# First stage of a hybrid encoder layer: mean squares from a second reading of x, and the heads' norm a tile later

## The chip, the cores and the metric

The kernel runs on one core of a Trainium2 chip, with no other core in use. The metric is the device time of one execution in microseconds, lower is better. A core has a matrix engine (TensorE, PE in the profile, with its weight loads as PEld), a vector engine (VectorE, DVE), a scalar engine (ScalarE, ACT), a general engine (GpSimd, POOL), and SyncE (SP), which here only issues transfers. Each engine works off a queue of its own in order, and they meet through semaphores. Sixteen DMA engines move the data between the chip's memory and the on-chip buffers.

## The reference

One layer of an encoder is applied to two sequences, of 2048 and 256 tokens, each token with 1024 values. The part that matters here is its beginning:

```
n = x * rsqrt(mean(x*x) + eps) * norm1_w
p = n @ w_in         # 4 x 512 columns for the matrix memory (mLSTM), 32 gates, 512 + 128 + 128 for q, k, v
q = rmsnorm per head of 64 (q) * q_norm_w ;  k likewise with k_norm_w
q, k = q*cos + rotated(q)*sin, ...             # axial rotary embedding
```

After it follow a bidirectional matrix memory with eight heads, softmax attention with eight query heads and two key heads, an output projection, a second norm, a gated convolution network, and a last norm. All values are float32.

## The kernel before, in words

Tokens are cut into 18 tiles of 128: tiles 16 and 17 belong to the short sequence and come first, then 0 to 15. The first stage is `phase_a`. It makes, for each tile, the attention's q, k and v and the gates (800 columns of w_in). The other columns are projected later, by the matrix memory's part, from a copy of the split x that the first stage leaves in memory.

To keep float32 accuracy with a faster form of the matrix product, every operand is split into a rounded half and a remainder; a product is then three matrix products. x is held transposed (`xT`: values on the partitions, tokens along the row), as the matrix product wants it. It is not normalised before the product: since the norm is one factor for each token, it is multiplied in afterwards, when the accumulators are read.

For one tile, the steps and their lines are:

- `front_a` (L184 to L189): SP issues the load of the transposed x, 512 KB, into one of three buffers.
- `front_b` (L191 to L198): ScalarE copies x into the rounded half (L195), VectorE makes the remainder (L196), and SP stores both, 1 MB (L197). Three tiles of the result `nT` are kept.
- `front_c` (L200 to L213): the mean square of each token. ScalarE squares x (L204), GpSimd adds the eight blocks of 128 values in three steps (L207 twice, L208), TensorE multiplies the sum by a vector of ones (L210), which adds over the partitions and puts the result on the tokens, VectorE adds eps (L212), GpSimd raises to the power -1/2 (L213). The result is a column of `g.rc`.
- `mm` (L244 to L258): 48 matrix products into an accumulator tile `pj` of two banks, of which there are two.
- `post_a` (L260 to L278): ScalarE reads q and k out of the accumulators with the token's factor (L264) into `qk`, of which there are two, and v (L267); VectorE makes v's remainder (L268) and the gates (L272); SP stores v (L270). ScalarE squares q and k (L275), VectorE sums for each head (L277), GpSimd adds eps and raises to -1/2 (L104, L105 in the helper `rstd_of`).
- `post_b` (L280 to L303): VectorE multiplies by the head's factor (L283) and applies the rotation in seven operations (L292, L296, L298), ScalarE and VectorE split the result (L300, L301), SP stores the queries (L302).
- `post2` (L332 to L338): TensorE turns the two key halves (L336), ScalarE copies them out (L337) and stores them from its own queue (L338).
- `gates` (L305 to L330): the forget gates' logarithms, for some tiles at a time, and their turn on TensorE (L329).

The loop at L357 sets the order in which the program is written. In iteration n it has `mm` of tile n, `post2` of tile n-1, `post_a` of n, `front_b` and `front_c` of n+3, `post_b` of n, some gate steps, some of the rotation's tables (`tables2`, on GpSimd, L241), one part of the next stage's weights (`wm`), and the load of x for n+4. A block under `tc.issue_after(ins)` adds, for each of its instructions on the engine of `ins`, that it is issued behind `ins`. The order in which each engine's queue is finally laid out comes from the framework's scheduler, which follows the written order as priority, but brings forward what it takes to be ready. After the loop come `gate_math`, the matrix memory's projections (`mj` at L780, `mv` at L790) and the attention, which are interleaved. The accumulators `pj` of the first stage make room for those of the projections.

Two parts of the matrix memory's code serve as rows for costs: L941 squares with a running sum on ScalarE, and L777 loads the stored split x back.

Of the kernel before, what the change touches and what calls it, by code (L numbers as in the profile page):

```python
# [9 lines left out]
F32 = mybir.dt.float32  # L10
F32R = mybir.dt.float32r
AF = mybir.ActivationFunctionType
# [141 lines left out]
def phase_a(g, tc, sw, st_x, after_x, after_mm, after_pj, wm):  # L154
# [3 lines left out]
    with ExitStack() as st:  # L158
# [32 lines left out]
        def front_b(i):  # L191

            nT = nTs[i] = sf.tile([P, NCC, 2, P], F32R, tag="nT", name=f"n1T{i}", bufs=3)
            x = xs[i]
            nc.scalar.activation(nT[:, :, 0, :], x, AF.Copy)  # L195
            ins = nc.vector.tensor_tensor(nT[:, :, 1, :], x, f32(nT[:, :, 0, :]), ALU.subtract)  # L196
            g.st.dma_start(g.n1_d[i // 2, :, :, i % 2], f32(nT))  # L197
            return ins  # L198

        def front_c(i):  # L200

            x = xs.pop(i)
            xq = sx.tile([P, NCC, P], F32, tag="xq", name=f"xq{i}", bufs=2)
            nc.scalar.activation(xq, x, AF.Square, scale=1.0 / 32.0)  # L204
            sq = sf.tile([P, P], F32, tag="sq", name=f"sq{i}")
            for k in (4, 2):
                nc.gpsimd.tensor_tensor(xq[:, 0:k], xq[:, 0:k], xq[:, k:2 * k], ALU.add)  # L207
            nc.gpsimd.tensor_tensor(sq, xq[:, 0], xq[:, 1], ALU.add)  # L208
            ps = pp.tile([P, 2], F32, tag="rs", name=f"rs_a{i}", bufs=2)
            nc.tensor.matmul(ps, sq, g.ones, start=True, stop=True)  # L210
            r = g.rc[:, i:i + 1]
            nc.vector.tensor_scalar(r, ps[:, 0:1], EPS, None, ALU.add)  # L212
            nc.gpsimd.tensor_tensor(r, r, g.mhalf[:, 0:1], ALU.pow)  # L213

        def weights(cs):
# [44 lines left out]
        def post_a(i, pj):  # L260

            qk = sp.tile([P, 10, HD], F32, tag="qk", name=f"qk{i}")
            rc = g.rc[:, i:i + 1]
            nc.scalar.activation(qk, pj[:, 0:640].rearrange("p (h d) -> p h d", d=HD), AF.Copy, scale=rc)  # L264
            v = sp.tile([P, 2, 2, HD], F32R, tag="v", name=f"v{i}", bufs=2)
            pv = pj[:, 640:768].rearrange("p (h d) -> p h d", d=HD)
            nc.scalar.activation(v[:, 0], pv, AF.Copy, scale=rc)  # L267
            nc.vector.scalar_tensor_tensor(v[:, 1], pv, rc, f32(v[:, 0]), ALU.mult, ALU.subtract)  # L268
            for a in range(2):
                g.st.dma_start(g.v_d[a, :, :, i].rearrange("g p d -> p g d"), f32(v[:, a]))  # L270
            gt = g.gtm[:, i]
            nc.vector.scalar_tensor_tensor(gt, pj[:, 768:800].rearrange("p (a k) -> p a k", a=2), rc,  # L272
                                           bgb.rearrange("p (a k) -> p a k", a=2), ALU.mult, ALU.add)
            xq = sp.tile([P, 10, HD], F32, tag="t2", name=f"qkq{i}", bufs=2)
            nc.scalar.activation(xq, qk, AF.Square, scale=0.125)  # L275
            ms = sp.tile([P, 10], F32, tag="ms10", name=f"ms10_{i}")
            nc.vector.tensor_reduce(ms, xq, AX.X, ALU.add)  # L277
            return qk, rstd_of(g, sp, ms, 10, f"rqk{i}")  # L278

        def post_b(i, qk, r):  # L280

# [70 lines left out]
        front_c(order[2])  # L352
        tables2(slice(0, 2))
        front_a(order[3])
        prev = None
        steps = []
        for n, i in enumerate(order):  # L357
            pj, = mm(i)
            if n:
                post2(order[n - 1], prev)  # L360
            if n == NT - 1:
                st_f.close()
                after_mm()
            qk, r = post_a(i, pj)
            with ExitStack() as behind:
                if n + 3 < NT:
                    behind.enter_context(tc.issue_after(front_b(order[n + 3]).ins))
                    front_c(order[n + 3])
                    if n + 4 == NT:
                        st_x.close()  # L370
                        after_x()
                prev = post_b(i, qk, r)
                if steps:
                    for _ in range(2 if n == NT - 1 else 1):
                        next(steps[0], None)
                if n < 7:
                    tables2(slice(2 * n + 2, min(2 * n + 4, NT1)))
                if wm:
                    wm.pop(0)()
            if n + 4 < NT:  # L380
                front_a(order[n + 4])
            if n == NT - 1:
                st_j.close()
                after_pj()
            if n % 4 == 1:
                for _ in (steps.pop() if steps else ()):
                    pass
                steps = [gates(*((NT1, 2) if n == 1 else (i - 3, 4)))]
                next(steps[0])
        for _ in steps[0]:  # L390
            pass
        post2(order[-1], prev)
# [1368 lines left out]
def layout(inputs):  # L1761
# [4 lines left out]
    def col(v):  # L1766
# [4 lines left out]
    w_m = np.concatenate([w_m[:LASTP], w_m[LASTP:][:, :, :, [1, 2, 0, 3]]], axis=0)  # L1771
    arrays = {
        "xT": x.reshape(NT, P, NCC, P).transpose(0, 3, 2, 1),
        "w_a": np.concatenate([w_in[:, ACOL + 32:ACOL + 800], w_in[:, ACOL:ACOL + 32]], axis=1).reshape(NCC, P, 800),
        "w_m": w_m.reshape(4, NCC, P, 512),
        "w_up": inputs["w_up"][0].reshape(NCC, P, 2 * NFC, P).transpose(2, 1, 0, 3),
# [26 lines left out]
```

## Time and profile before

| what | value |
|---|---|
| median of three runs | 3371.0 us (3368.56 to 3371.91) |
| span of the profiled execution, the one time that is shown of it | 3372.4 us |
| TensorE busy, whole span | 97% |
| first projection of the first stage starts | 8.35 us |
| first projection of the matrix memory (L780) starts | 208.21 us |
| mean granted TensorE clock, whole span | 0.986 |

The profile is that of one execution. A row of a busy-time view gives a stretch's bounds, then for each engine the microseconds it was busy and the number of instructions, the mean clock that TensorE was granted (1.00 is full), the share of the DMA engines that was busy, and the rate. A row of the waits names who waited, for what, then the total, how often, and the longest, in microseconds. A row of the groups gives line, engine, operation, output and inputs, shapes and count, then the total busy time and the mean of one in nanoseconds, then the idle time before it and who ended it. A row of the order of time gives start, length, engine, line, and in brackets the idle time of the engine before it. A row on one source line gives shortest, middle and longest duration in nanoseconds, then the first and last start.

### The profile page before, as it was taken

What the parts mean: (1) busy time and instruction counts of PE and PEld (TensorE: products, weight loads), DVE (VectorE), ACT (ScalarE), POOL (GpSimd) and SP (SyncE); (2) the same over time, 40 slices, a digit from 0 to 9 for tenths busy, and PEclk for the clock granted to TensorE, in tenths of its full rate; (3) what the DMA queues carried; (4) which work ended last, traced back from release to release, by engine and by line L of the source; (5) the groups of instructions that cost most, each with busy time, mean ns of one, the idle gap of its engine ahead of it and who ended that gap; (6) DMA issues with size and microseconds to landing.
All of it is one profiled execution on the core that took longest, in us unless ns stands there. A gap on an engine that the chain in (4) does not pass through costs nothing. (4 is left out here: it accounts for less than half of the span.)

```text
span 3372.4 us, 57131 instructions
## 1 busy us (share of the span) xinstructions
PE 3271.5 (97%) x21366; PEld 3047.6 (90%) x21366; DVE 2403.1 (71%) x3727; ACT 1802.4 (53%) x3781; POOL 1327.6 (39%) x1686
## 2 busy tenths in 40 slices
PE   8899999999999999899999999999999999999998
PEld 6788888888888888788889999999999998999998
DVE  7875687777768788876766778877877776544573
ACT  5545666667666777665552544445555555323331
POOL 8652133213333323211246457645554442851112
PEclk9999999999999999999999999999999999999999
DMA  8765343343336444433347334424322223885563
GB/s 273 229 201 150 94 126 97 105 125 98 113 108 188 130 135 128 123 99 96 103 133 263 129 102 148 127 96 176 107 93 97 100 93 102 302 274 172 164 223 107
DMA packets 300636, 483.03 MB, mean 143 GB/s; under 512 B 36597, under 2 KB 186279, under 8 KB 300359
## 3 DMA queue, kind: packets, MB, share of 16 engines
q1 hardware_dynamic: 247543, 348.34, 32.8%
q0 software_dynamic: 36256, 121.60, 10.8%
q10 hardware_dynamic: 16560, 9.44, 0.9%
q8 instruction: 168, 2.75, 0.3%
q14 instruction: 109, 0.89, 0.1%
HBM read 337.37 MB, written 141.91 MB: 142 GB/s over the span
## 5 line engine op out<-in xcount | busy, mean ns | idle before, releaser
L622 DVE TENSOR_TENSOR pl<-ps,ph 128x512 fp32r<-128x512 f32 x520 | 354.0, 685 | 202.1 <-ACT ps L621 190.3
L1226 PE MATMUL pa<-nt,wut 128*128 128x290 f32 (+1 forms) x3168 | 449.2, 298 | 8.7 <-ACT u L1244 8.6
L620 ACT ACTIVATE ph<-ps 128x512 fp32r<-128x512 f32 x520 | 310.0, 596 | 265.7 <-PE ps L617 253.1
L1226 PEld LDWEIGHTS pa<-nt,wut 128*128 128x128 f32 x3168 | 433.1, 190 | 10.9 <-ACT u L1244 10.6
L591 DVE TENSOR_REDUCE mx<-px 128x1 f32<-128x512 f32 (+1 forms) x528 | 346.5, 674 | 100.0 <-PE px L590 98.0
L1336 DVE SCALAR_TENSOR_TENSOR y<-u,cw,y 128x1152 f32<-128x1152 f32 (+1 forms) x176 | 325.3, 1848 | 39.2 <-ACT yc L1334 17.5
L634 PE MATMUL pv<-ph,v 128*128 128x512 f32 (+1 forms) x1040 | 319.4, 402 | 0.8 <-ACT ph L620 0.3
L621 ACT ACTIVATE ps<-ps 128x512 f32<-128x512 f32 x520 | 310.3, 597 | 0.0
L1555 PE MATMUL et<-tet,wet 128*128 128x384 f32 x1584 | 279.0, 336 | 0.0
L1555 PEld LDWEIGHTS et<-tet,wet 128*128 128x128 f32 x1584 | 277.1, 188 | 0.0
L1069 PEld LDWEIGHTS po<-cmx,wo 128*128 128x128 f32 x1728 | 221.6, 191 | 9.6 <-DVE cmx L1057 1.5
L1069 PE MATMUL po<-cmx,wo 128*128 128x256 f32 x1728 | 225.8, 284 | 1.5 <-DVE cmx L1057 1.3
L1555 PE MATMUL e<-te,we 128*128 128x384 f32 x1188 | 213.9, 341 | 11.0 <-ACT te L1397 7.1
L1555 PEld LDWEIGHTS e<-te,we 128*128 128x128 f32 x1188 | 211.5, 191 | 12.0 <-ACT te L1397 7.3
L616 PE MATMUL ps<-qq,kk 128*128 128x512 f32 x520 | 215.9, 417 | 6.0 <-DVE mx L591 3.8
L780 PE MATMUL mj<-mn,wm 128*128 128x256 f32 x1296 | 200.8, 289 | 9.7 <-DMA mn<-n_d 3.9
L780 PEld LDWEIGHTS mj<-mn,wm 128*128 128x128 f32 x1296 | 185.5, 194 | 26.6 <-issue 6.8
L617 PE MATMUL ps<-qm,kl 65*128 65x512 f32 x520 | 207.6, 401 | 0.0
L590 PE MATMUL px<-kk,qq 128*128 128x512 f32 (+1 forms) x528 | 203.2, 415 | 3.9 <-DVE mx L591 2.6
L790 PEld LDWEIGHTS mv<-wm,mn 128*128 128x128 f32 x1296 | 181.9, 190 | 17.8 <-ACT qb L786 2.3
L790 PE MATMUL mv<-wm,mn 128*128 128x256 f32 x1296 | 194.8, 285 | 0.9 <-ACT qb L786 0.8
L634 PE MATMUL pv<-pl,v 128*128 128x512 f32 x520 | 192.2, 401 | 0.0
(307 smaller groups left out, 7216.9 us busy)
## 6 DMA issues: line engine op xcount, KB each, us to landing
mn<-n_d SPq DMA_DIRECT2D x216, 256.0 KB, 3.4
ru<-w_up SPq DMA_DIRECT2D x88, 512.0 KB, 3.6
a_d<-y POOLq DMA_DIRECT2D x88, 288.0 KB, 2.6
a_d<-tc POOLq DMA_DIRECT2D x66, 288.0 KB, 2.8
n_d<-n1T SPq DMA_DIRECT2D x18, 1024.0 KB, 5.7
dm<-nm_d POOLq DMA_DIRECT2D x72, 256.0 KB, 4.0
mjn<-n_d SPq DMA_DIRECT2D x72, 256.0 KB, 3.5
mvn<-n_d SPq DMA_DIRECT2D x72, 256.0 KB, 3.1
```

Of the source, the lines that this page charges most:

```text
L591: nc.vector.tensor_reduce(s.mx[:, t, z0:z0 + 1], ps[:, 0:w], AX.X, ALU.max)
L616: nc.tensor.matmul(ps, kk[:, kc:kc + P], s.qq[:, 0:N], start=True, stop=False)
L620: nc.scalar.activation(ph, ps, AF.Exp)
L621: nc.scalar.activation(ps, ps, AF.Exp)
L622: nc.vector.tensor_tensor(pl, ps, f32(ph), ALU.subtract)
L634: nc.tensor.matmul(s.pv[0:HD if k in (1, 3) else P, 0:N], v, p, start=(kp == 0 and k == 0), stop=(2 * kp + 2 == s.nk and k == 5))
L780: nc.tensor.matmul(pj[:, o], s.w[c][:, a, o * P:(o + 1) * P], nT[c][:, :, h, :], start=(c + o + k == 0), stop=(c == NCC - 1 and k == 2 and ...
L790: nc.tensor.matmul(pv[:, o], nT[c][:, o, a, :], s.w[c][:, h, 256:512], start=(c + o + k == 0), stop=(c == NCC - 1 and k == 2 and o == 1))
L1069: nc.tensor.matmul(po[:, o], wo[z // 2][c][:, a, n], mx[c][:, h, :], start=(c == 0 and k == 0), stop=(c == NCC - 1 and k == 2))
L1226: nc.tensor.matmul(p[:, z], w[:, aa, c, :], ops[k][:, c, bb, z * m:z * m + m], start=c == 0 and i == 0 and not add, stop=c == NCC // 2 - 1 ...
L1336: nc.vector.scalar_tensor_tensor(y[:, s:e], u[:, s + k:e + k], cw[:, k, jj:jj + 1], y[:, s:e], ALU.mult, ALU.add)
L1555: nc.tensor.matmul(ps[m // 2][:, m % 2], w[:, aa, m * P:(m + 1) * P], t[:, bb], start=p == 0 and n == 0, stop=p == NP - 1 and n == 2)
```

## The change

The host also hands in x as it is, token-major (`xn`, 18 tiles of 128 tokens by 1024 values). `front_c` loads that tile on SP's queue (512 KB), ScalarE squares it in place and gives the sum over the row as an accumulated output straight into the column of `g.rc`, and GpSimd adds eps and raises to the power. The three additions of GpSimd, the product with ones and VectorE's addition are gone. x in its transposed form is now read by `front_b` alone.

The loop runs `post_b` of tile n-1 in iteration n, behind the sum over the heads of tile n on VectorE, and `post2` of tile n-2. After the loop the last tile's `post_b` and the last two `post2` follow.

```
         def front_b(i):
...
-            x = xs[i]
+            x = xs.pop(i)
...
         def front_c(i):
-            x = xs.pop(i)
-            xq = sx.tile([P, NCC, P], F32, tag="xq", name=f"xq{i}", bufs=2)
-            nc.scalar.activation(xq, x, AF.Square, scale=1.0 / 32.0)
-            sq = sf.tile([P, P], F32, tag="sq", name=f"sq{i}")
-            for k in (4, 2):
-                nc.gpsimd.tensor_tensor(xq[:, 0:k], xq[:, 0:k], xq[:, k:2 * k], ALU.add)
-            nc.gpsimd.tensor_tensor(sq, xq[:, 0], xq[:, 1], ALU.add)
-            ps = pp.tile([P, 2], F32, tag="rs", name=f"rs_a{i}", bufs=2)
-            nc.tensor.matmul(ps, sq, g.ones, start=True, stop=True)
+            xn = sx.tile([P, D], F32, tag="xn", name=f"xn{i}", bufs=2)
+            nc.sync.dma_start(xn, g.xn[i])
             r = g.rc[:, i:i + 1]
-            nc.vector.tensor_scalar(r, ps[:, 0:1], EPS, None, ALU.add)
+            nc.scalar.activation(xn, xn, AF.Square, scale=1.0 / 32.0, accum_out=r)
+            nc.gpsimd.tensor_scalar(r, r, EPS, None, ALU.add)
             nc.gpsimd.tensor_tensor(r, r, g.mhalf[:, 0:1], ALU.pow)
...
-            nc.vector.tensor_reduce(ms, xq, AX.X, ALU.add)
-            return qk, rstd_of(g, sp, ms, 10, f"rqk{i}")
+            last = nc.vector.tensor_reduce(ms, xq, AX.X, ALU.add)
+            return qk, rstd_of(g, sp, ms, 10, f"rqk{i}"), last.ins
...
-            if n:
-                post2(order[n - 1], prev)
+            if n > 1:
+                post2(order[n - 2], prev)
...
-            qk, r = post_a(i, pj)
+            qk, r, last = post_a(i, pj)
...
-                prev = post_b(i, qk, r)
+                if n:
+                    with tc.issue_after(last):
+                        prev = post_b(order[n - 1], *behind_a)
+                behind_a = qk, r
...
+        post2(order[-2], prev)
+        prev = post_b(order[-1], *behind_a)
         for _ in steps[0]:
             pass
         post2(order[-1], prev)
```

More of the change, by code (lines that the diff above doesn't have):

```diff
@@ L354, in phase_a @@
         front_a(order[3])
-        prev = None
+        prev = behind_a = None
         steps = []
@@ L1773, in layout @@
         "xT": x.reshape(NT, P, NCC, P).transpose(0, 3, 2, 1),
+        "xn": x.reshape(NT, P, D),
         "w_a": np.concatenate([w_in[:, ACOL + 32:ACOL + 800], w_in[:, ACOL:ACOL + 32]], axis=1).reshape(NCC, P, 800),
```

## The prediction

> **What bounds the kernel now.** I read the page first: the span, and the busy shares of the engines.
>
> ```profile
> span 3372.4 us, 57131 instructions
> PE 3271.5 (97%) x21366; PEld 3047.6 (90%) x21366; DVE 2403.1 (71%) x3727; ACT 1802.4 (53%) x3781; POOL 1327.6 (39%) x1686
> ```
>
> TensorE is busy 97% of the span, so over the whole kernel the bound is TensorE and a change pays only where it shortens TensorE's own work or its idle time. The span is the only time that is shown of this profiled execution; it lies 1.4 us (0.04%) above the 3371.0 us median of the three runs, which is small against the steps below, so I make the sum against 3372.4 us and give the result as it comes out. The changed code runs only in the first stage. There I read the busy time by stretch, second.
>
> ```profile
> core 0: us, PE busy (x) PEld busy (x) DVE busy (x) ACT busy (x) POOL busy (x), PEclk, DMA share, GB/s
> 0.00:20.00 20.00, 11.01 (x46) 9.13 (x47) 13.24 (x12) 13.91 (x15) 11.73 (x19) 1.00 0.92 309
> 20.00:60.00 40.00, 36.93 (x193) 31.64 (x192) 27.68 (x54) 18.07 (x26) 35.59 (x47) 0.96 0.87 287
> 60.00:110.00 50.00, 42.50 (x235) 36.86 (x233) 40.31 (x73) 27.72 (x45) 38.83 (x36) 0.97 0.67 214
> 110.00:160.00 50.00, 44.12 (x231) 37.75 (x232) 40.39 (x82) 27.13 (x49) 30.64 (x28) 0.94 0.73 237
> 160.00:205.00 45.00, 44.58 (x257) 38.72 (x255) 36.89 (x78) 22.18 (x44) 25.72 (x27) 0.99 0.67 224
> ```
>
> Three things stand in it. From 20 to 205 us TensorE is idle for 3.07 + 7.50 + 5.88 + 0.42 = 16.9 us. The granted clock takes (1 - 0.96) x 40 + (1 - 0.97) x 50 + (1 - 0.94) x 50 + (1 - 0.99) x 45 = 6.5 us more. And the DMA engines are nowhere idle: their share is 0.87, 0.67, 0.73, 0.67, after 0.92 at the start. After 160 us TensorE hardly waits, so what there is to win lies before. Third I read what ended TensorE's idle time in the first 205 us.
>
> ```profile
> PE rs_a L210 <- POOL sq L208: 6.3, 4, 2.7
> PE pk L336 <- DVE qz L301: 3.7, 3, 1.7
> PE pj L254 <- DVE gtm L320: 3.2, 1, 3.2
> PE pj L254 <- DVE gtm L272: 1.9, 2, 1.6
> PE pg L329 <- ACT kT L337: 1.4, 1, 1.4
> ```
>
> These five are 16.5 of the 16.9 us. The first is the sums of squares: the tiny matmul against ones stands in TensorE's queue behind a projection and waits for GpSimd's additions. The second is the keys' turn waiting for the rotated heads. The next two are a projection that waits until VectorE has read the accumulators of two tiles earlier.
>
> **Removed: the sums of squares on GpSimd and TensorE.** Here are the groups of GpSimd from 20 to 205 us.
>
> ```profile
> L105 POOL TENSOR_TENSOR rqk<-rqk,mhalf 128x10 f32<-128x10 f32 x17 | 37.1, 2181 | 1.0
> L207 POOL TENSOR_TENSOR xq<-xq 128x512 f32<-128x512 f32 x16 | 25.4, 1594 | 7.7 <-ACT xq L204 7.7
> L207 POOL TENSOR_TENSOR xq<-xq 128x256 f32<-128x256 f32 x16 | 16.7, 1051 | 0.6
> L213 POOL TENSOR_TENSOR rc<-rc,mhalf 128x1 f32<-128x1 f32 x17 | 15.4, 908 | 19.0 <-DVE rc L212 19.0
> L104 POOL TENSOR_SCALAR rqk<-ms 128x10 f32<-128x10 f32 x17 | 11.3, 664 | 24.0 <-DVE ms L277 23.5
> L208 POOL TENSOR_TENSOR sq<-xq 128x128 f32<-128x128 f32 x16 | 10.0, 630 | 0.6
> ```
>
> The three additions cost 1.594 + 1.051 + 0.630 = 3.3 us for each tile, 52 us over the stretch. They go, and a small addition of 128x1 comes in, between 0 and the 0.66 us of the 128x10 one; I take 0.5 us. GpSimd is off TensorE's path once nothing on TensorE waits for it, so its 2.8 us a tile count through the waits alone: the 6.3 us go entirely, because the matmul itself goes. That matmul's own slots go too.
>
> ```profile
> 77.48 0.28 PE L210 MATMUL rs_a<-ones,sq 128*128 128x2 f32 x2
> 77.62 2.11 PE L254 MATMUL pj<-w_a,n1T 128*128 128x512 f32 x8
> ```
>
> From its start to that of the next projection is 0.14 us, where it waited for nothing. Eighteen tiles make 2.5 us of TensorE time, all on the path.
>
> GpSimd's additions also cost VectorE time.
>
> ```profile
> L283 DVE TENSOR_TENSOR xh<-qk,rqk x18: 817/826/1918, 43.4 to 218.4; 128x640 f32<-128x640 f32 x18
> DVE xh L283 <- POOL rqk L105: 25.0, 16, 3.6
> ACT qk L264 <- DVE xh L283: 19.0, 8, 5.2
> ```
>
> The multiply by the heads' norm takes 0.82 us, but up to 1.92 us when an addition of GpSimd runs beside it. VectorE also stands 25.0 us waiting for the heads' power on GpSimd, and ScalarE 19.0 us behind that. VectorE is at 145 of 185 us (27.68 + 40.31 + 40.39 + 36.89), so both are what makes it late.
>
> **Moved: norm, rotation and keys' turn a tile later.** Before, VectorE's queue holds norm and rotation of a tile (which wait for GpSimd) ahead of the next tile's reading of its accumulators. Now the reading comes first, then the previous tile's rotation, whose power was finished a tile ago. So the 25.0 us wait goes, the accumulators are released early (3.2 + 1.9 us of TensorE), and the turn stands on TensorE behind a projection more (3.7 us). All that the moved part issues moves with it: nine operations on VectorE, one on ScalarE, the query store on SP's queue, and in the later half two transposes, a copy and a store on ScalarE's queue. Their number is unchanged. What is late next: the buffer of the heads' values has two places, so reading tile n needs the norm of tile n-2, which now runs one iteration closer to it. With VectorE no longer waiting that has most of a tile to spare; if VectorE lags, the 19.0 us row stays. The wait of 1.4 us (a transpose of the gates behind a copy) has no part in it and stays.
>
> **The clock.** The halved clock follows the waits, as two short stretches show.
>
> ```profile
> 61.00:63.50 2.50, 0.00 (x0) 0.00 (x0) 2.50 (x4) 0.00 (x0) 2.50 (x3) 1.00 0.45 143
> 65.00:68.00 3.00, 3.00 (x12) 2.62 (x11) 2.10 (x6) 3.00 (x6) 3.00 (x2) 0.50 0.98 253
> ```
>
> TensorE is idle for the wait of 2.7 us on the squares, and soon after runs at 0.50. If the waits go, the 6.5 us go with them. The Trainium skill, page "TensorE: Matmul & The Clock Gate" (Part 1 and "HAM oscillation"), has the gate fall back after an idle window of about 3.4 us and advises against gaps above that; by it waits of 1.7 to 2.7 us would cost no clock, and of the 6.5 us only those behind the one 3.2 us wait, at most 3.0 us, might go. The rows decide here: a gap below 3 us was followed by half clock.
>
> **The end of the stage.** The matrix-memory projections start late.
>
> ```profile
> 204.48 0.38 PE L329 MATMUL pg<-ident,gp 128*40 128x128 f32 x2
> 205.43 0.36 ACT L267 ACTIVATE v<-pj,rc 128x128 fp32r<-128x128 f32 x1
> 207.72 0.23 DVE L268 SCALAR_TENSOR_TENSOR v<-pj,rc,v 128x128 fp32r<-128x128 f32 x1
> 207.87 0.24 DVE L272 SCALAR_TENSOR_TENSOR gtm<-pj,rc,bgb 128x32 f32<-128x32 f32 x1
> 208.21 1.05 PE L780 MATMUL mj<-mn,wm 128*128 128x256 f32 x4 [3.35 <-issue]
> ```
>
> They begin 0.1 us after VectorE's last reading of the last accumulators, which stood behind the rotation of the tile before. Now that rotation follows it, so it can start at 205.8 instead of 207.7: 1.8 us. On the other side one rotation more (about 6 us of VectorE) now comes after the loop, ahead of the last gates; the projections cover it, since they need neither. If that cover were gone it would cost those 6 us.
>
> **Added: the second reading of x.** ScalarE squares the same 1024 elements, and its running sum must be read out. The trace has that form further down, in the heads' norm of the matrix memory.
>
> ```profile
> L204 ACT ACTIVATE xq<-x 128x1024 f32<-128x1024 f32 x15 | 15.6, 1055 | 11.5 <-POOL sq L208 6.4 <-DMA x<-xT 3.8 <-POOL rqk L104 1.3
> L941 ACT ACTIVATE s<-hh x144: 238/248/311, 443.7 to 1433.7; 128x64 f32<-128x64 f32 x144
> L941 ACT ACTIVATION_READ_ACCUMULATOR s<-hh x144: 187/192/258, 443.8 to 1433.8; 128x1 f32 x144
> ```
>
> So 0.19 us for each tile, 3.5 us on ScalarE in all, hidden: it is busy 95.1 of 185 us. The square no longer waits for GpSimd (6.4 + 1.3 us), but it now waits for a load of its own, with qk, v and everything else of ScalarE queued behind it, and TensorE behind those.
>
> ```profile
> x<-xT SPq DMA_DIRECT2D x16, 512.0 KB, 6.6
> SPq L270 <- ACT v L267: 27.7, 9, 4.6
> 34.46 1.06 ACT L195 ACTIVATE n1T<-x 128x1024 fp32r<-128x1024 f32 x1 [1.59 <-DMA x<-xT]
> ```
>
> The like load of x takes 6.6 us to land. The new one can be issued when its buffer (two places) is free, two tiles ahead; but SP's queue is in order and stands 27.7 us behind the value stores alone. A 524 KB load costs the DMA engines, at the 237 GB/s for a share of 0.73 (325 GB/s for a full one), 1.6 us; eighteen cost 29 us. At the start three of them lie ahead of the fourth tile's x, which ScalarE already waited 1.59 us for: that is 0 to 4.8 us later.
>
> **The sum.** What can go at most from 20 to 205 us is 6.3 + 3.7 + 3.2 + 1.9 of waits, 2.5 of slots and 6.5 of clock: 24.1 us. What the DMA engines allow is less. From 20 to 160 us they are busy 34.8 + 33.5 + 36.5 = 104.8 us; some fifteen new loads add 24: 129 of 140 us, which is the 0.92 of the fullest stretch shown. At that share the stretch does not shrink at all, unless stores slip into the 45 us after it, which have room for (0.92 - 0.67) x 45 = 11 us; then it can shrink by about 12. Between 0 and 12 I take 8, since the stores are what can slip (three tiles of n are kept, and the waits removed came from engines, not from DMA). With 1.8 us at the end the gain is 10 us: 3372.4 - 10 = 3362 us. TensorE being the bound afterwards, it should reach the end of the kernel.
>
> **Rivals.** *The DMA engines take the place of GpSimd* (chance 0.28): the stretch keeps its 140 us, loads of x come late, only the end's 1.8 us and some 2 us after 160 remain: 3368 us, from 3364 to 3374. For it speaks the 0.87 from 20 to 60 us; against it that TensorE's rows name no DMA there.
>
> *ScalarE's queue stands behind the new load* (0.16, the slower side): if SP issues the load only when its own tile's turn comes, ScalarE waits up to 6.6 us a tile. It has 90 us free over the 17 tiles from 20 to 205 us, 5.3 us each; beyond that each microsecond is TensorE's. It decides once load and square together leave less than those 5.3 us: 1.3 us x 17 = 22 us slower, 3394; with the 10 us gained set against it, 3384. Against it: nothing keeps the load from being issued two tiles ahead.
>
> *Nearly everything goes* (0.12): DMA keeps up, 24.1 and the end's 3.35 us go: 3345 us. Against it the DMA sum above.
>
> **Chances.** The forecast case, 3357 to 3366 us, has 0.44. A difference of 0.2%, 6.7 us, is about what a measurement here can tell. Faster than that takes in nearly all of the forecast and the third rival; within it lie most of the DMA rival and the forecast's upper edge: 0.53, 0.31, 0.16. From 3349 to 3376 us the range leaves out most of the last rival and most of the slower one.
>
> **What would show it.** Right: no wait of TensorE on GpSimd in the first stage, 0.99 or more of clock from 60 to 160 us, VectorE's multiply near 0.82 us throughout and not waiting for the power, DMA share above 0.8 there, matrix-memory projections before 200 us. Wrong: ScalarE's square waiting for the second reading for over 20 us in all, or TensorE's projections ending idle time on n1T or on a DMA; then the DMA rival or the slower one holds. Also wrong if the stage ends earlier and the last instruction does not.

## The result and the profile after

The changed kernel takes 3351.6 us (median of four runs, 3349.3 to 3356.0) against 3369.8 us of the kernel before (median of four, 3364.7 to 3371.9). The ratio is 0.9948, with a 95% interval of 0.9936 to 0.9960: 18.2 us, or 0.5%, faster. The forecast was 10 us. The two profiled executions lie further apart than the medians, 3348.6 against 3372.4 us of span, which is 23.8 us: before's profiled execution has a span of 3372.4 us, longer than each of its four timed executions (3371.9 at most). A step by step account within the profiles therefore has to explain 23.8 us, and a statement on the kernels 18.

The head of the page first: span, and busy time, share and instructions of each engine.

```profile
span 3348.6 us, 57051 instructions
PE 3261.4 (97%) x21330; PEld 3037.4 (91%) x21330; DVE 2373.6 (71%) x3709; ACT 1803.6 (54%) x3799; POOL 1267.4 (38%) x1650
```

TensorE has 36 instructions fewer (two passes for each of the 18 products with ones), GpSimd 36 fewer and 60 us less, VectorE 18 fewer. None of that is 24 us of TensorE: its busy time fell by 10.1 us and the span by 23.8, so more than half of it was idle time. The busy time by stretch shows where (columns as in the prediction).

```profile
0.00:20.00 20.00, 12.13 (x52) 9.94 (x53) 11.00 (x11) 12.27 (x13) 2.01 (x13) 1.00 0.91 331
20.00:60.00 40.00, 36.43 (x195) 31.18 (x194) 25.51 (x59) 21.53 (x34) 27.51 (x43) 0.96 1.04 360
60.00:110.00 50.00, 49.30 (x272) 42.73 (x271) 41.56 (x87) 34.43 (x62) 25.80 (x25) 1.00 1.05 368
110.00:160.00 50.00, 49.69 (x284) 43.39 (x284) 38.52 (x90) 33.49 (x62) 22.41 (x23) 1.00 0.93 304
160.00:205.00 45.00, 41.45 (x283) 38.35 (x283) 29.36 (x64) 22.71 (x54) 22.14 (x49) 0.96 0.67 216
```

From 60 to 160 us TensorE is busy 98.99 of 100 us at full clock, where it was busy 86.62 at 0.97 and 0.94. From 20 to 60 us nothing was won: 36.43 us against 36.93. In the first 20 us TensorE is busy 1.1 us more (12.13 against 11.01), which the prediction had not counted. The DMA engines stand at 1.04 and 1.05, above the 0.92 that the prediction took for full. What ended TensorE's idle time in the first 205 us:

```profile
PE pj L248 <- ACT w_a L112: 7.4, 1, 7.4
PE pj L248 <- ACT n1T L195: 2.2, 1, 2.2
PE mj L779 <- ACT og L795: 2.2, 1, 2.2
PE pj L248 <- DVE gtm L266: 1.9, 3, 1.0
PE mv L789 <- ACT qb L785: 1.3, 1, 1.3
```

The first row is the start of the kernel and was there before (8.3 us). No row names GpSimd any more, nor the keys' turn. Two of the rows belong to the matrix memory, which now begins inside this window. In order of time, TensorE's end of the stage:

```profile
178.79 1.58 PE L248 MATMUL pj<-w_a,n1T 128*128 128x288 f32 x10
180.21 1.59 PE L779 MATMUL mj<-mn,wm 128*128 128x256 f32 x12
```

The projection of the matrix memory follows that of the first stage without a gap, at 180.21 us instead of 208.21. These 28.0 us hold the whole gain; 4.2 us of them are lost again by the end of the span. VectorE's waits and its multiply by the heads' factor (min, median, max in nanoseconds, then first and last start):

```profile
DVE xh L277 <- POOL rqk L105: 1.8, 1, 1.8
```

```profile
L277 DVE TENSOR_TENSOR xh<-qk,rqk x18: 811/818/1027, 45.9 to 189.9; 128x640 f32<-128x640 f32 x18
```

The wait for the power fell from 25.0 us to 1.8, and the multiply takes 0.82 us throughout, 1.03 at most, where it took up to 1.92. ScalarE pays for it as follows, in its groups from 20 to 205 us and in its waits of the first 205 us.

```profile
L205 ACT ACTIVATE xn<-xn 128x1024 f32<-128x1024 f32 x17 | 17.9, 1052 | 4.0 <-DMA xn<-xn 2.6 <-ACT kT L331 0.9 <-DMA rm<-w_m 0.4
L205 ACT ACTIVATION_READ_ACCUMULATOR xn<-xn 128x1 f32 x17 | 3.2, 188 | 0.0
```

```profile
ACT n1T L195 <- DMA x<-xT: 3.3, 3, 2.7
ACT xn L205 <- DMA xn<-xn: 2.9, 4, 2.1
ACT qk L258 <- DVE xh L277: 1.1, 1, 1.1
```

The running sum costs 0.19 us a tile, as the row from the matrix memory said. ScalarE waits for the second reading four times, 2.9 us in all, and its 19.0 us behind the multiply are 1.1.

### The profile page after: what moved, and what is told of

Same layout as the page of the kernel before. It is cut to its first block, busy times and chain, and to the rows that moved or that the text cites. A ratio compares the mean times of both kernels' runs of the same rounds, so it can differ in the third digit from the quotient of the medians.

```text
span 3348.6 us, 57051 instructions
## 1 busy us (share of the span) xinstructions
PE 3261.4 (97%) x21330; PEld 3037.4 (91%) x21330; DVE 2373.6 (71%) x3709; ACT 1803.6 (54%) x3799; POOL 1267.4 (38%) x1650
## 5 line engine op out<-in xcount | busy, mean ns | idle before, releaser
L1225 PEld LDWEIGHTS pa<-nt,wut 128*128 128x128 f32 x3168 | 433.7, 190 | 10.1 <-ACT u L1243 8.6
L1554 PE MATMUL e<-te,we 128*128 128x384 f32 x1188 | 213.4, 340 | 11.5 <-ACT te L1396 7.1
```

The costliest lines, as they stand in the source:

```text
L1225: nc.tensor.matmul(p[:, z], w[:, aa, c, :], ops[k][:, c, bb, z * m:z * m + m], start=c == 0 and i == 0 and not add, stop=c == NCC // 2 - 1 ...
L1554: nc.tensor.matmul(ps[m // 2][:, m % 2], w[:, aa, m * P:(m + 1) * P], t[:, bb], start=p == 0 and n == 0, stop=p == NP - 1 and n == 2)
```

## The experiments

The theory after reading the two traces: TensorE's idle time came from chains in queues that are worked off in order. TensorE's tiny product stood behind GpSimd's additions, and the token's factor, the reading of the accumulators and the turn stood behind the power and the rotation. The change takes the chains apart; the DMA engines could bear the new loads. Three rivals: it is GpSimd's work as such that made VectorE late; the new loads now bound the stage, so that without them there would be more to win; the two halves of the change each bring their own part. Each kernel is the changed one with one edit, except where the text says otherwise. Ratios are to the kernel before, and a ratio of 0.001 is 3.4 us. Differences from the change come from ratios or from medians, which agree within 3 us, so smaller ones mean nothing.

**The squares alone: e1_squares_only.** The kernel before with the new `front_c`; norm, rotation and turn stay where they were.

```
-                if n:
-                    with tc.issue_after(last):
-                        prev = post_b(order[n - 1], *behind_a)
-                behind_a = qk, r
+                prev = post_b(i, qk, r)
```

> Only the mean squares are changed (second reading, running sum); norm, rotation and turn stay in their own tile's iteration. Theory A (the squares' chain over GpSimd and TensorE was the larger loss): the 6.3 us of waits on the squares, 2.5 us of slots and about half of the 6.5 us of clock go, 10 to 13 us faster than before, and 4 to 6 us of TensorE's waits on the rotated heads and on the reading of the accumulators stay. Rival B (VectorE's queue, with rotation ahead of the reading, was the larger loss): 0 to 5 us faster, the waits on the accumulators' reading grow in place of those on the squares. Rival C (the DMA engines take the place): within 4 us of before, with waits on x.

Measured: 3352.4 us, ratio 0.9947 (0.9933 to 0.9961). That is the whole gain of the change. Of TensorE's waits the two that the move was to take are still there:

```profile
PE pj L248 <- DVE gtm L266: 2.9, 3, 1.6
PE pk L330 <- DVE qz L295: 2.1, 2, 1.8
```

and VectorE still waits 13.7 us for the power, but TensorE is busy 47.83 and 48.92 of 50 us from 60 to 160. The reading of x from memory is enough by itself. It brought more than theory A's 10 to 13 us, though the waits that theory A left standing, 5.0 us, were in its range of 4 to 6.

**The move alone: e2_move_only.** The change with the old `front_c`: squares of the transposed x, GpSimd's additions, the product with ones.

```
-            xn = sx.tile([P, D], F32, tag="xn", name=f"xn{i}", bufs=2)
-            nc.sync.dma_start(xn, g.xn[i])
...
+            nc.tensor.matmul(ps, sq, g.ones, start=True, stop=True)
```

> Only norm, rotation and turn are moved a tile later; the mean squares stay with GpSimd and TensorE. Theory A: the waits on the rotated heads and on the accumulators' reading go (8.8 us with the clock behind them perhaps 10), those on the squares stay at 6 us or grow: 3 to 8 us faster than before. Rival B: 10 to 18 us faster. A third possibility: GpSimd, with the head's power and the additions, is late all the same and the buffer of the heads' values, of two places, makes ScalarE wait: no faster or slower.

Measured: 3357.7 us, ratio 0.9966 (0.9952 to 0.9979), so some 11.5 us of gain. With 18 us for the squares alone and 17.5 for both, the halves overlap for the larger part: they relieve the same lateness, and whichever comes first takes most of it. The product with ones waits less, though nothing was done to it:

```profile
PE pj L254 <- DVE t L314: 3.2, 1, 3.2
PE rs_a L210 <- POOL sq L208: 2.3, 2, 1.8
```

2.3 us instead of 6.3. So part of what the prediction booked on the squares belonged to the queues that both edits shorten. The first row is again a reading of the accumulators, which ends at 50.8 us behind a rotation on VectorE; the move, which was to take such waits, leaves this one. The time lies in the range of rival B (10 to 18 us) and outside that of theory A (3 to 8), while for e1 rival B had only 0 to 5. Neither holds for both runs: which half is the larger loss has no answer, because they overlap. This counts against the rival with a part of its own for each half.

**No second load: e3_no_second_load.** The square always takes the first tile's values, from a buffer that stays; 17 loads go, and every token gets the factor of the first tile's.

```
-            xn = sx.tile([P, D], F32, tag="xn", name=f"xn{i}", bufs=2)
-            nc.sync.dma_start(xn, g.xn[i])
+            if not xns:
+                xns.extend(sx.tile([P, D], F32, tag="xn", name=f"xn{k}", bufs=2) for k in range(2))
+                nc.sync.dma_start(xns[0], g.xn[i])
```

> The changed kernel without the second reading: ScalarE squares the first tile's values each time, into a buffer of its own, so that seventeen loads of 512 KB are left out and every token gets a factor of the first tile. If the DMA engines have become the bound of the first stage, as the forecast had it (share 1.04 from 20 to 110 us), the stage ends several us sooner: 5 to 10 us faster than the changed kernel. If the loads are hidden, the time is within 3 us of the changed kernel; the wait of TensorE at 36 us, on the fourth tile's x, should go in either case.

Measured: 3351.8 us, ratio 0.9940 (0.9924 to 0.9956), which cannot be told from the change.

```profile
20.00:60.00 40.00, 34.86 (x181) 29.82 (x180) 26.91 (x60) 31.24 (x56) 34.74 (x58) 0.96 0.93 303
60.00:110.00 50.00, 50.00 (x288) 44.12 (x287) 43.31 (x94) 29.09 (x53) 30.98 (x18) 1.00 0.94 302
110.00:160.00 50.00, 50.00 (x285) 43.65 (x284) 38.07 (x80) 28.57 (x51) 17.31 (x12) 1.00 0.74 242
```

The share of the DMA engines falls to 0.94 and 0.74, and TensorE is busy all of the 100 us, 1.0 us more than with the loads. From 60 to 160 us no more can be won: TensorE is the bound. The early wait behind x at 36 us went too, but in its place stands another of 5.0 us on the reading of the accumulators (two waits, the longest 4.5). That they cost 5 to 10 us, as the expectation had it for full DMA engines, is not so: the loads cost nothing that shows in the time.

**More to load: e4_load_more, e5_small_load_more, e10_copy_more.** If the loads are free, how far is it to where they are not? Three kernels move more per tile: 256 KB more into a one-place buffer, 32 KB more into the same, and a copy of 512 KB from memory to memory, which needs no buffer and for which nothing waits.

```
+            xe = sx.tile([P, D // 2], F32, tag="xe", name=f"xe{i}", bufs=1)
+            nc.sync.dma_start(xe, g.xn[i, :, 0:D // 2])
```

> The changed kernel with a third reading of half the size: for each tile 256 KB more, which nothing uses, behind the second reading on SP's queue. 4.7 MB at the 360 GB/s of the changed kernel are 13 us of the DMA engines. If these are the bound from 20 to 110 us, about half of the tiles' loads show: 6 to 13 us slower than the changed kernel. If there is room left, within 3 us.

Measured: 3366.8 us, ratio 0.9994 (0.9983 to 1.0005), 15 us more than the change. This one does not tell bytes from buffers. The extra loads stand in SP's queue up to 201.9 us, their buffer space is kept as long, and the matrix memory's first load waits behind:

```profile
206.65 1.65 PE L781 MATMUL mj<-mn,wm 128*128 128x256 f32 x6 [3.54 <-DMA mn<-n_d]
```

The projection of the matrix memory begins at 206.65 us, waiting for that load, nearly as late as in the kernel before, although the stage's own projections end at 187.2 us, 7 us later than in the change. The small load has the same buffer and the same place in the queue, with an eighth of the bytes:

```
+            xe = sx.tile([16, D // 2], F32, tag="xe", name=f"xe{i}", bufs=1)
+            nc.sync.dma_start(xe, g.xn[i, 0:16, 0:D // 2])
```

> The changed kernel with the same additional transfer for each tile at the same place of SP's queue as the run with 256 KB more, but of 32 KB alone (16 partitions), so 0.6 MB in all. If the bytes on the DMA engines made that run 15 us slower than the changed kernel, this one is within 3 us of the changed kernel. If the issuing on SP's queue, the wait for the one buffer or another order of the queues did it, this one is slower by 8 us or more too.

Measured: 3356.4 us, ratio 0.9958 (0.9941 to 0.9974). The 3.4 us over the change lie within the intervals. The wait behind the matrix memory's load is there, at 192 us:

```profile
PE pj L250 <- DVE gtm L268: 5.6, 3, 3.7
PE mj L781 <- DMA mn<-n_d: 4.1, 2, 3.7
```

So the place in the queue alone costs a few microseconds at most, and the rest of e4's 15 comes with the size: the bytes (18 x 262 KB, 13 us at 360 GB/s) or the longer wait for a larger buffer. The copy asks for the bytes without a buffer:

```
-            nc.sync.dma_start(xn, g.xn[i])
+            ld = nc.sync.dma_start(xn, g.xn[i])
+            with tc.issue_after(ld.ins):
+                nc.sync.dma_start(g.xc_d[i], g.xn[i])
```

> The changed kernel with a copy of each tile of the token-major x from memory to memory (512 KB read and 512 KB written), right behind the second reading on SP's queue; nothing uses or waits for it, and no buffer on the core is held, so it loads the DMA engines alone. Eighteen copies are about 9.4 MB, 26 us at the changed kernel's 360 GB/s. If the DMA engines have no room left between 20 and 160 us (share 1.04, 1.05, 0.93), 15 to 30 us slower than the changed kernel. If there is room, within 5 us; then what slowed the run with 256 KB more was its buffer, which the next stage waited for, and not the bytes.

Measured: 3377.8 us, ratio 1.0028 (1.0018 to 1.0038), 27 us more than the change and 9 more than the kernel before.

```profile
20.00:60.00 40.00, 34.79 (x180) 29.27 (x180) 24.94 (x56) 22.53 (x35) 28.05 (x43) 0.96 1.06 375
60.00:110.00 50.00, 39.03 (x192) 33.30 (x191) 33.35 (x73) 23.91 (x45) 21.34 (x18) 0.86 1.05 371
110.00:160.00 50.00, 44.31 (x245) 38.73 (x245) 28.97 (x61) 26.43 (x50) 16.39 (x18) 0.97 0.86 287
```

The rate from 20 to 110 us rises only from 360 and 368 GB/s to 375 and 371, the share hardly, and TensorE has 39.03 busy us of 50 where it had 49.30. Eighteen copies of 524 KB are 9.4 MB, at 360 GB/s 26 us, about what the run lost. From 110 to 160 us the share is 0.86, so the engines are full in the earlier part only; TensorE's last idle time in the stage ends before 150 us. From 20 to 110 us the changed kernel has the DMA engines full, and from 60 us on TensorE too. Seventeen loads fewer bring nothing, eighteen transfers more cost about all that they last. How e4's 15 us divide between bytes and buffer stays open, but bytes alone can cost as much.

**GpSimd's additions, in the chain and beside it: e6_additions_kept, e11_additions_apart.** Both keep three additions of the old sizes on GpSimd, with an unused result. In e6 they read the squared values, so that they stand behind the square and ahead of the token's factor in GpSimd's queue, where the old ones stood.

```
+            xe = sx.tile([P, 512], F32, tag="xe", name=f"xe{i}", bufs=1)
+            nc.gpsimd.tensor_tensor(xe, xn[:, 0:512], xn[:, 512:1024], ALU.add)
+            nc.gpsimd.tensor_tensor(xe[:, 0:256], xe[:, 0:256], xe[:, 256:512], ALU.add)
+            nc.gpsimd.tensor_tensor(xe[:, 0:128], xe[:, 0:128], xe[:, 128:256], ALU.add)
```

> The changed kernel with GpSimd's three additions back on each tile, on the squared values and into a buffer that nothing reads: GpSimd's load, its delay of the powers and its cost to VectorE are back, the product with ones and TensorE's wait for it are not. If what counted was GpSimd's load (late head's power, slow VectorE), half or more of the gain goes: 8 to 15 us slower than the changed kernel. If what counted was TensorE's own queue (product and wait), within 4 us of the changed kernel.

Measured: 3370.8 us, ratio 1.0009 (0.9999 to 1.0019): the gain is gone, more than the 8 to 15 us expected. ScalarE now waits for the token's factor, and TensorE for the accumulators:

```profile
ACT qk L262 <- POOL rc L211: 36.5, 10, 5.5
```

```profile
PE pj L252 <- DVE gtm L270: 8.4, 7, 2.6
```

They also keep the second reading's buffer longer, but that is not it: ScalarE's square waits 2.0 us in all for that load, less than in the change. In e11 the same work stands behind the power and reads the split x, which is there long before; nothing waits for it.

```
+            xe = sf.tile([P, 4, P], F32, tag="xe", name=f"xe{i}", bufs=1)
+            n = f32(nTs[i])[:, :, 0, :]
+            nc.gpsimd.tensor_tensor(xe, n[:, 0:4], n[:, 4:8], ALU.add)
+            nc.gpsimd.tensor_tensor(xe[:, 0:2], xe[:, 0:2], xe[:, 2:4], ALU.add)
+            nc.gpsimd.tensor_tensor(xe[:, 0], xe[:, 0], xe[:, 1], ALU.add)
```

> The changed kernel with GpSimd's three additions back, on the tile's rounded x and behind the power of the token's factor in the written order, with a buffer that nothing reads: GpSimd's load and its cost to VectorE are back, but no buffer of the second reading is held and no product waits. If GpSimd's load is what the gain came from, 8 to 15 us slower than the changed kernel, as with the additions on the squares (19 us slower). If there the held buffer and the late factor did it, within 4 us.

Measured: 3355.5 us, ratio 0.9959 (0.9944 to 0.9974), 3.7 us over the change, which the intervals hardly separate. The collision with VectorE is back:

```profile
L282 DVE TENSOR_TENSOR xh<-qk,rqk x18: 807/818/1899, 44.2 to 196.1; 128x640 f32<-128x640 f32 x18
```

```profile
60.00:110.00 50.00, 45.77 (x242) 39.45 (x241) 48.42 (x81) 30.76 (x56) 43.65 (x42) 0.93 1.00 334
```

One multiply takes 1.90 us again, VectorE is busy 48.42 of 50 us and GpSimd 43.65, and TensorE is still 45.77 against 42.50 in the kernel before. The same additions cost some 20 us where the token's factor stands behind them and about 4 where nothing does. The rival with GpSimd's work as such falls as the main cause. A small part may be left: in e11 a projection waits 4.2 us for the accumulators at 73 us, and the matrix memory's projections begin at 186.42 us, 6.2 us later than in the change.

**The product with ones: e12_product_kept, e13_place_kept.** In e12 the product comes back alone: one block of the squared values against ones, result unused.

```
+            ps = pp.tile([P, 2], F32, tag="rs", name=f"rs_a{i}", bufs=2)
+            nc.tensor.matmul(ps, xn[:, 0:P], g.ones, start=True, stop=True)
```

> The changed kernel with a product with ones back on TensorE for each tile, on a part of ScalarE's squares, result unused: TensorE's slots (0.14 us each, 2.5 us) and its waiting for ScalarE's square are back, GpSimd's additions are not. If TensorE's queue standing behind the squares was a main loss, 6 to 12 us slower than the changed kernel; if the lateness came from GpSimd, the square is ready when the product's turn comes, and it is 2 to 5 us slower.

Measured: 3364.9 us, ratio 0.9991 (0.9980 to 1.0002), 13 us more than the change. That is much more than 18 slots and above both ranges of the expectation. In order of time one of them, and the end of the stage:

```profile
177.90 0.28 PE L207 MATMUL rs_a<-ones,xn 128*128 128x2 f32 x2
178.04 2.81 PE L250 MATMUL pj<-w_a,n1T 128*128 128x512 f32 x15
...
181.31 2.10 PE L250 MATMUL pj<-w_a,n1T 128*128 128x288 f32 x14
...
185.20 1.69 PE L781 MATMUL mj<-mn,wm 128*128 128x256 f32 x12
...
255.11 1.22 PE L781 MATMUL mj<-mn,wm 128*128 128x256 f32 x4 [5.04 <-DMA mn<-n_d]
```

The slot is 0.14 us, as forecast. Only one product waits (2.5 us, for the square). The stage's projections end at 183.4 us instead of 180.4, the matrix memory's begin at 185.2, 5.0 us later than in the change, and at 255 us the latter wait 5.0 us for a load of the stored x. From 180 to 300 us TensorE waits for such loads 8.1 us in all, against 2.2 in the change, but its idle time of all kinds is only 4.2 us more (105.8 us busy against 109.9). The profiled spans differ by 11.9 us; the later start and that idle time overlap in part and make at most 9.2 of it. Another explanation was left: the product's result keeps two places in the accumulator memory, and what follows the stage might get its own later. In e13 the places are kept to the end of the stage, but only the first tile's product is made.

```
-            ps = pp.tile([P, 2], F32, tag="rs", name=f"rs_a{i}", bufs=2)
-            nc.tensor.matmul(ps, xn[:, 0:P], g.ones, start=True, stop=True)
+            if i == order[0]:
+                ps = [pp.tile([P, 2], F32, tag="rs", name=f"rs_a{k}", bufs=2) for k in range(2)]
+                nc.tensor.matmul(ps[0], xn[:, 0:P], g.ones, start=True, stop=True)
```

> The change with the product against ones made for the first tile only (result unused, on one block of the squared values), but with both places of its result kept in the accumulator memory to the end of the stage. e12_product_kept, with all eighteen products, took 3364.9 us against 3351.6 of the change, far more than 18 slots of 0.14 us. If the eighteen products on TensorE's queue are what costs there (slots, a 2.5 us wait, and an order of the following work that is shifted by them), this run stands near the change: 3350 to 3354 us, ratio 0.994 to 0.996. If the places kept are what costs (what follows the stage gets its accumulators later), it stands near the other: 3361 to 3366 us, ratio 0.998 to 1.000, with the matrix memory's projections waiting near 185 or 250 us.

Measured: 3348.6 us, ratio 0.9946 (0.9933 to 0.9960), the change's time. So it is the seventeen further products, not their places. But e12 brings back more than slots in TensorE's queue: its product reads the second reading's buffer, so that the load two tiles on waits in SP's queue until TensorE has come to the product.

```profile
SPq L203 <- PE rs_a L207: 10.3, 6, 4.9
```

ScalarE's square does not wait longer for its load (1.7 us against 2.9), but the last square starts at 178.1 us instead of 164.8, and ScalarE waits 13.6 us for the token's factor, against 6.5 in the change. No run of the changed kernel has the products without this tie. So why the insertion costs 13 us is shown only in part: 3 us in the stage, the rest in the interleaved work behind it, whose order comes out differently. What belongs to the slots, to the tie between the queues and to chance of the order stays open.

**One place for the second reading: e7_one_buffer.** The slower rival needed loads that come only when their own tile's turn comes. One place instead of two makes that case.

```
-            xn = sx.tile([P, D], F32, tag="xn", name=f"xn{i}", bufs=2)
+            xn = sx.tile([P, D], F32, tag="xn", name=f"xn{i}", bufs=1)
```

> The changed kernel with one buffer for the second reading in place of two: a load can be issued only when the square of the tile before is done. This is the mechanism of the slower rival, ScalarE's queue behind the load. If ScalarE has room, the wait of the square on its load grows to 2 to 4 us a tile, and the time stays within 5 us of the changed kernel, since the queue's other work was placed ahead; if the rival's price holds, 10 to 30 us slower.

Measured: 3361.5 us, ratio 0.9979 (0.9970 to 0.9987), 10 us slower than the change.

```profile
ACT xn L205 <- DMA xn<-xn: 22.1, 10, 5.9
ACT qk L258 <- POOL rc L207: 12.0, 8, 5.4
```

```profile
PE pj L248 <- DVE gtm L266: 9.1, 1, 9.1
```

ScalarE waits 22.1 us for the load where it waited 2.9, the token's factor comes late, and TensorE stands 9.1 us once. The profiled execution was the slowest of the eleven (3367.6 us), so the single long wait may be more than the usual. The mechanism of that rival is real, at 1.2 us a tile instead of the 2 to 4 expected, and the second place is what keeps it away.

**The early wait: e9_tables_x_early.** The wait at 36 us is for the fourth tile's x, whose load stands behind the tables' and the new readings. Here that load is issued ahead of the tables, and GpSimd's table work behind the power of the heads.

```
+        front_a(order[3])
...
-        front_a(order[3])
...
-                    tables2(slice(2 * n + 2, min(2 * n + 4, NT1)))
+                    with tc.issue_after(g.power):
+                        tables2(slice(2 * n + 2, min(2 * n + 4, NT1)))
```

> A version to beat the changed kernel: the rotation's tables on GpSimd are issued behind the head's power of their own iteration, in place of ahead of it, and the fourth tile's x is loaded before the tables and before the third tile's second reading. In the changed kernel TensorE is idle 3.6 us and at half clock for 3.4 us between 20 and 60 us, first for the fourth tile's x at 36 us, then for the reading of the accumulators behind GpSimd at 49 us. If both causes are named rightly, these go: 3 to 6 us faster than the changed kernel. If the DMA engines are what limits the start, the wait only moves: within 2 us.

Measured: 3350.0 us, ratio 0.9948 (0.9936 to 0.9961), no better than the change. The first wait is gone (0.5 us left) and a like one stands 30 us later:

```profile
PE pj L248 <- ACT v L261: 2.7, 1, 2.7
```

TensorE is busy 38.95 of 40 us from 20 to 60 (36.43 in the change), but 46.38 of 50 from 60 to 110 (49.30). Just before, from 53 to 60 us, ScalarE's queue stood 7.2 us behind a transfer, where it stood 3.3 us in the change. This fits DMA engines that are full in both stretches (1.04 and 1.03), where a transfer brought forward is another put back. The edit moved GpSimd's table work too, so the reading is argued and not shown.

## Why the prediction was right, and where it was not

The direction was right, the waits that were named went, and the time lies in the range. But 3351.6 us is outside the forecast case (3357 to 3366) and nearer to the third rival's 3345 than to the 3362 of the sum; it lies 2.6 us inside the range's fast end, so that the range holds it is in part luck. The size of one term was wrong, and so was the division of the gain between the two edits.

**The waits, the slots and the clock.** The prediction counted 24.1 us that could go from 20 to 205 us, and 3.35 us at the stage's end: 27.5 us. The matrix memory's first projection came 28.0 us earlier, 1.1 of them from the first 20 us. So nearly all of it went. Single items differ: 1.9 us behind the gates' reading are left, and a new wait of 2.2 us behind x came in. The division between the edits was wrong too. The prediction gave 6.3 us of waits, 2.5 of slots and a share of the clock to the squares and the rest to the move; e1 and e2 show that either edit alone takes most of the same time (18 and 11.5 us of 17.5).

**The DMA ceiling: the failed term.** The prediction took "the 0.92 of the fullest stretch shown" for what the DMA engines can bear, got 129 of 140 us from it, and cut 24.1 us to "between 0 and 12", of which it took 8. The stretches ran at 1.04, 1.05 and 0.93, and at 360 and 368 GB/s against the 325 it had worked out for a full share. 1.04 x 40 + 1.05 x 50 + 0.93 x 50 = 140.6 us of share went into the 140 us: the new loads and, since the stage runs ahead, some transfers of what follows. The stretch shrank by nearly all there was. The trace of before would have shown that 0.92 is not the ceiling: it was a mean over the first 20 us, in which the transfers were only starting. Its DMA engines over the first 205 us in 40 slices, busy tenths and rate:

```profile
DMA  5999799796868859495936976397909491837994
GB/s 172 394 385 287 218 378 378 208 318 240 250 228 226 298 167 337 129 280 198 292 124 207 304 232 234 100 315 240 294 18 311 163 344 46 302 129 217 350 341 171
```

The first slice has half a share and 172 GB/s; the second and third have 394 and 385 GB/s. And three microseconds in which TensorE waits for the squares, in the busy times by stretch:

```profile
46.00:49.00 3.00, 0.71 (x6) 0.47 (x4) 3.00 (x4) 2.98 (x5) 3.00 (x4) 1.00 1.05 399
```

Share 1.05 at 399 GB/s. At 1.05 the prediction's own 129 us fit into 123, so that 17 us could go without any transfer slipping, and the 45 us behind have room for (1.05 - 0.67) x 45 = 17 more: the ceiling would not have cut the 24.1 us. Yet the concern was not idle: e10 shows that from 20 to 110 us hardly any DMA time was left.

**The three rivals.** That nearly everything goes had 0.12 and gave 3345 us: its picture is the one that the profile shows, 3348.6 us in the profiled execution. The DMA rival fell with the ceiling. The slower one exists (e7), but the reason given against it held: the load is issued two tiles ahead, and ScalarE waits 2.9 us, not 22.

**The end of the stage.** Forecast were 1.8 us of the 3.35; all of it went, since the last projection is followed at once by that of the matrix memory. Forecast was also that the gain reaches the end of the kernel: 23.8 of 28.0 us do. From 160 to 205 us TensorE has 3.55 idle us and a clock of 0.96, where it had 0.42 and 0.99; the matrix memory's start waits there for ScalarE (2.2 and 1.3 us), which it did later before.

**The early loads.** The prediction had the fourth tile's x come 0 to 4.8 us later. ScalarE waited 2.68 us for it and began at 37.27 us, 2.8 us later than before, and TensorE waited 2.2 us behind that. So this stretch won nothing. A wait of a projection on n1T was one of the prediction's signs of being wrong, and it came (2.2 and 0.3 us), though neither rival that it stood for holds; the sign beside it, 20 us of ScalarE behind the second reading, did not come.

**Small prices.** The read-out of the running sum was 0.188 us as forecast; GpSimd's new addition took 0.41 us against the 0.5 taken; ScalarE's 3.2 us are hidden.

**The clock.** Forecast was 0.99 or more from 60 to 160 us; it was 1.00. What is left follows the waits that are left. In the change, the busy time around the wait at 36 us:

```profile
36.00:38.00 2.00, 0.14 (x2) 0.00 (x0) 0.00 (x0) 0.73 (x1) 1.84 (x6) 1.00 1.04 426
38.60:42.00 3.40, 3.06 (x7) 1.91 (x7) 3.40 (x4) 2.95 (x3) 3.32 (x4) 0.50 1.06 353
42.00:46.00 4.00, 4.00 (x18) 3.19 (x17) 2.21 (x4) 1.80 (x4) 3.92 (x4) 1.00 1.01 302
```

and in e9_tables_x_early, where the wait stands at 65 us:

```profile
65.00:68.00 3.00, 0.59 (x5) 0.36 (x3) 2.97 (x9) 2.69 (x6) 1.88 (x2) 1.00 1.02 397
68.00:71.00 3.00, 2.68 (x8) 2.14 (x9) 2.93 (x6) 2.98 (x5) 2.92 (x4) 0.64 1.07 381
```

A wait of 2.2 us is followed by 3.4 us at half clock, and when the wait moves, the half clock moves with it: the 20 to 60 us stretch of e9 has 1.00. The page of the Trainium skill that the prediction weighed, "TensorE: Matmul & The Clock Gate" (Part 1), has the gate fall back after an idle window of about 3.4 us; here gaps of 2.2 and 2.7 us were enough, so the rows were rightly preferred. But not every such gap is followed so. In e13_place_kept TensorE is idle from 199.0 to 201.2 us, as long as at 36 us in the change, and then has

```profile
201.20:204.60 3.40, 3.36 (x28) 3.37 (x29) 3.13 (x1) 0.50 (x2) 0.00 (x0) 1.00 1.04 391
```

full clock. So the length of a gap of about 2.2 us does not settle whether it costs clock; what does is not shown here.

## What to carry to other kernels

A small instruction in an in-order queue is priced by what it waits for and by what stands behind it, not by its length: the same three additions cost 20 us ahead of the token's factor and about 4 apart. Eighteen products of 0.14 us cost 13 us, for reasons that the runs show only in part. Paying for a shorter chain with a second reading of the same data is good as long as the transfer engines have room; read that room from the share in the fullest short stretch, not from a mean in which transfers are only starting. When two edits relieve the same lateness, their gains are not added, and one of them may be left out.

## What the runs showed of the hardware

The share of the DMA engines can stand above 1 for long: 1.04 to 1.06 over 40 to 50 us, at 360 to 375 GB/s. That was the ceiling here, since 9.4 MB more on top raised the rate by 4% at most and cost 27 us. In shorter stretches a share of 1.01 to 1.06 went with rates from 302 to 426 GB/s, so it is the share that tells how full the engines are. In the kernel before, 5 of the 18 multiplies of 128x640 on VectorE took 1.9 us instead of 0.82; each of the five began within 0.2 us after the start of one of GpSimd's 128x512 additions. One such multiply came back in e11, where the kernel lost nothing that could be measured surely. Half clock, for 3.4 us, followed gaps of TensorE of 2.2 to 2.7 us, but not each of them.
